# Choosing sixteen experts a head from 112 sums instead of 256, with one lookup for both keys

## The chip, the cores and the metric

The kernel runs on one core of a Trainium2 chip. The metric is the device time of one execution in microseconds (us); the time before is the median of three runs. A second source of numbers is one profiled execution of the same program, with its own time.

The engines are named as in the profile: PE (matrix multiplications, with PEld for their weight loads), DVE (vector engine), ACT (scalar engine), POOL, and SP, whose queue issues the weight transfers.

## The reference, cut to what matters

Two transformer blocks run on 256 tokens of width 1024. The second ends in a mixture of 16,384 experts, each a row of `expert_u` and a row of `expert_v`. For each of 8 heads a token has two lists of 128 scores; an expert is a pair of places, one of each list, and its score is the sum.

```python
def peer_ffn(h, w_pq, sub_keys, expert_u, expert_v):
    ...
        q = (hb @ w_pq).reshape(TOK_BLOCK, PEER_HEADS, 2, PEER_DHALF)
        s = jnp.einsum('thpd,hpnd->thpn', q, sub_keys).astype(jnp.float32)
        s1, i1 = lax.top_k(s[:, :, 0], PEER_TOPK)        # 16 best of 128
        s2, i2 = lax.top_k(s[:, :, 1], PEER_TOPK)
        cand_s = (s1[..., :, None] + s2[..., None, :]).reshape(TOK_BLOCK, PEER_HEADS, PEER_TOPK * PEER_TOPK)
        cand_i = (i1[..., :, None] * N_KEYS + i2[..., None, :]).reshape(...)
        top_s, pos = lax.top_k(cand_s, PEER_TOPK)        # 16 best of 256 sums
        idx = jnp.take_along_axis(cand_i, pos, axis=-1)
        gate = jax.nn.softmax(top_s, axis=-1).astype(hb.dtype)
        u = expert_u[idx]
        act = jax.nn.gelu(jnp.einsum('thkd,td->thk', u, hb), approximate=False)
        vv = expert_v[idx]
        return jnp.einsum('thk,thkd->td', gate * act, vv)
```

Both lists come out sorted, best first. A sum of place a of the first list and place b of the second is beaten or equalled by every sum at places no later in both lists.

## The kernel before

The kernel gathers no expert rows. It multiplies all experts with all tokens, and a dense matrix of gates (`GA`, 128 x 128 x 256: first key, second key, token) that is zero for experts that were not chosen does the selection.

**The stretch around the change.** After the first block and the attention and recurrence of the second, `lin_T(xs6, A["w_pq"], ...)` makes the queries in 16 column blocks (`evpq`, L1536, writes them to `qT`). `choose()` starts with 64 small multiplications (L1590) that give the 32 lists of scores (two halves of 128 tokens, `t`, times 8 heads times 2 keys), copied to `sc` by ACT (L1592). Then the loop over the experts begins: 64 calls of `u_pair(c, td)`, each with two slabs of 128 experts of `eu`. Later 64 pairs of slabs of `ev` follow.

**A slab.** `slab()` loads 512 KB to a buffer `raw` (three buffers), and `split()` makes two parts of it: `hi` on ACT (L327, three buffers) and `lo = raw - hi` on DVE (L329, two buffers). PE needs both: each slab of `eu` is 8 groups of three multiplications, `hi` by `hbh` (L336), `hi` by `hbl` (L337), `lo` by `hbh` (L338). A `raw` buffer is free for the next transfer when its `lo` is made.

**The choice.** `choose()` is a generator. It works on DVE alone except for its exponential, its final transposes and copies. For each half `t`:

- 16 lists: `top16` finds the 16 best of 128 and their places in five steps: MAX8 (L1560), FIND_INDEX8 (L1561), MATCH_REPLACE8 (L1562, into a scratch part of `tmp`), MAX8 (L1563), FIND_INDEX8 (L1564). In the chip each FIND and REPLACE has a short MATCH_VALUE_LOAD ahead of it.
- 8 heads: all 256 sums of the two lists (L1601), which need the two lists of that head only, and `top16` over them.
- The place of a sum, 0 to 255, is split into the two list places by a shift (L1609 or L1611) and a mask, each made into pairs of 16-bit numbers by a copy (L1612).
- The lookup of the key numbers, once for each of the two keys: compare with 0 to 15 (L1617, 2048 wide, 16 bit), multiply by the 16 key numbers (L1621), sum over 16 (L1622).

Then come the gates, and transposes and copies (`pk`, `pg`), and 32 calls of `g_group`, each of which puts the gates of 8 tokens into `GA`.

**What sets the order.** The program text interleaves the two streams: each `u_pair` is followed by up to `U_STEPS = 3` steps of `choose()` until it ends, then by as many `g_group` calls as spread 32 of them over the pairs left but for the last `U_LAST // 2`. The framework (`TileContext(nc, schedule_with_timeline_sim=True)`) turns this text into one fixed queue for each engine at compile time, with a timeline of its own; work that is ready may be put ahead of work that stands earlier in the text. On the chip each engine keeps that order. The scratch `tmp` is shared: what the second half writes there comes after what the first half's lookup does there.

Of the kernel before, what the change touches and what calls it, by code (L numbers as in the profile page):

```python
# [12 lines left out]
F16 = mybir.dt.float16  # L13
# [3 lines left out]
OP = mybir.AluOpType  # L17
AX = mybir.AxisListType
PSUM = bass.MemoryType.PSUM

P = 128
# [193 lines left out]
def body(tc, A, out):  # L215
    nc = tc.nc
    V, S, G, PE = nc.vector, nc.scalar, nc.gpsimd, nc.tensor
    es = ExitStack()
    with es:
# [14 lines left out]
        def pw(g=None):  # L234
            if g is None:
                turn[0] ^= 1
            return psw.tile([P, 512], F32, tag=f"w{turn[0] if g is None else g}", name=nm("w"), bufs=4 - LIN_PS // 2)
# [401 lines left out]
        while j < KC:  # L639
            n = 1  # L640
# [151 lines left out]
        n = MEM_PER  # L792
# [730 lines left out]
        GA = gap.tile([P, P, T], F32, name="GA")  # L1523
        view = lambda i, n, k: GA[:, i:i + n].rearrange("p a t -> p (a t)").rearrange("p (k t) -> p k t", k=k)
# [1 line left out]
        qT = GA[:, 112:128]  # L1526
        keys = view(104, 8, 16)
        sc = view(88, 16, 32)
        cand = view(72, 16, 16)
        tmp = view(64, 8, 8)  # L1530
        for j in range(2):
            nc.sync.dma_start(keys[:, 8 * j:8 * j + 8], A["keys"].rearrange("p (k n) -> p k n", k=16)[:, 8 * j:8 * j + 8])
# [12 lines left out]
        gp = es.enter_context(tc.tile_pool(name="gp", bufs=1, side="right", reuse_waits="tile"))  # L1545
# [4 lines left out]
        def carve(n, *dims):  # L1550
            flat = GA.rearrange("p a t -> p (a t)")[:, at_[0]:at_[0] + n]
            at_[0] += n
            names = "abcde"[:len(dims)]
            return flat.rearrange(f"p ({' '.join(names)}) -> p {' '.join(names)}", **dict(zip(names[:-1], dims[:-1])))

        v16 = carve(512, 2, 16, 16)
        u16 = carve(512, 2, 16, 16).bitcast(U32)

        def top16(src, scratch, vals, idx):
            V.max(vals[:, 0:8], src)  # L1560
            V.max_index(idx[:, 0:8], vals[:, 0:8], src)  # L1561
            V.match_replace(scratch, vals[:, 0:8], src, -3e38)  # L1562
            V.max(vals[:, 8:16], scratch)  # L1563
            V.max_index(idx[:, 8:16], vals[:, 8:16], scratch)  # L1564

        tv = carve(256, 2, 8, 16)
        tu = carve(256, 2, 8, 16).bitcast(U32)
        gs = carve(32, 2, 8, 2)
        ii = carve(768, 3, 2, 8, 16)
        assert at_[0] <= 64 * T  # L1570

        n16 = gp.tile([P, 2, 16, 16], F16, tag="o1", name="n16", bufs=2)
        ab = gp.tile([P, 2, 8, 16, 2], F16, tag="o1", name="ab", bufs=2)
        io = gp.tile([P, P], F16, name="io")
        G.iota(io, pattern=[[1, P]], base=0, channel_multiplier=0, allow_small_or_imprecise_dtypes=True)

# [3 lines left out]
        def twice(a):  # L1580
            return a.rearrange("p (g t) -> p g t", t=8)[:, :, :, None].to_broadcast([P, T // 8, 8, 2])

        def choose():

            for t in range(2):
                ts = slice(t * P, t * P + P)
                for g in range(4):
                    p_ = pw()
                    for i in range(4):
                        PE.matmul(p_[:, i * P:i * P + P], lhsT=qT[:, 4 * g + i, ts], rhs=keys[:, 4 * g + i], start=i == 0,  # L1590
                                  stop=i == 3, skip_group_check=True)
                    S.activation(sc[:, 16 * t + 4 * g:16 * t + 4 * g + 4], p_.rearrange("p (k n) -> p k n", k=4), AF.Copy)  # L1592
            yield
            for t in range(2):
                for k in range(16):
                    top16(sc[:, 16 * t + k], tmp[:, k % 8, 0:P], v16[:, t, k], u16[:, t, k])
                    yield
                V.tensor_copy(n16[:, t], u16[:, t])
                for h in range(8):
                    c = cand[:, 8 * t + h]  # L1600
                    V.tensor_tensor(c.rearrange("p (a b) -> p a b", a=16), v16[:, t, 2 * h, :, None].to_broadcast([P, 16, 16]),  # L1601
                                    v16[:, t, 2 * h + 1, None].to_broadcast([P, 16, 16]), op=OP.add)
                    top16(c, tmp[:, h], tv[:, t, h], tu[:, t, h])
                    yield

                pos = u16[:, t, 0:8]
                for s in range(2):
                    if s:
                        V.tensor_scalar(pos, tu[:, t], 15, None, op0=OP.bitwise_and)  # L1609
                    else:  # L1610
                        V.tensor_scalar(pos, tu[:, t], 4, None, op0=OP.logical_shift_right)  # L1611
                    V.tensor_copy(ab[:, s], pos[:, :, :, None].to_broadcast([P, 8, 16, 2]))  # L1612
                yield
                for s in range(2):
                    eq = tmp[:, 4 * s:4 * s + 4].bitcast(F16).rearrange("p a t -> p (a t)")
                    pairs = eq.rearrange("p (m a b) -> p m a b", a=8, b=2)
                    V.tensor_tensor(pairs, ab[:, s].rearrange("p h k b -> p (h k) b")[:, :, None].to_broadcast([P, P, 8, 2]),  # L1617
                                    io[:, None, 0:16].rearrange("p m (a b) -> p m a b", b=2).to_broadcast([P, P, 8, 2]),
                                    op=OP.is_equal)
                    four = eq.rearrange("p (h k a) -> p h k a", h=8, k=16)  # L1620
                    V.tensor_tensor(four, four, n16[:, t, s:16:2, None].to_broadcast([P, 8, 16, 16]), op=OP.mult)  # L1621
                    V.tensor_reduce(ii[:, s, t], four, axis=AX.X, op=OP.add)  # L1622
                    yield

            gt_ = ii[:, 2]
            V.tensor_tensor(gt_, tv, tv[:, :, :, 0:1].to_broadcast([P, 2, 8, 16]), op=OP.subtract)
            S.activation(gt_, gt_, AF.Exp)
            V.tensor_reduce(gs[:, :, :, 0], gt_, axis=AX.X, op=OP.add)
            V.reciprocal(gs[:, :, :, 1], gs[:, :, :, 0])
            V.tensor_tensor(gt_, gt_, gs[:, :, :, 1:2].to_broadcast([P, 2, 8, 16]), op=OP.mult)  # L1630
            yield
            for s in range(3):
                p_ = pw()
                for t in range(2):
                    PE.transpose(p_[:, t * P:t * P + P], ii[:, s, t].rearrange("p h k -> p (h k)"), ident)
                if s < 2:
                    S.activation(pk[:, :, s], twice(p_[:, :T]), AF.Copy)
                else:

                    S.activation(pg[:, :, 0], twice(p_[:, :T]), AF.Copy, scale=GS)  # L1640
                    V.scalar_tensor_tensor(pg[:, :, 1], twice(p_[:, :T]), GS, pg[:, :, 0], op0=OP.mult, op1=OP.subtract)
            yield
# [45 lines left out]


        steps = choose()  # L1690
        next(steps)
        ng, first = 0, None
# [70 lines left out]
```

## Time and profile before

| | us |
|---|---|
| median of 3 runs | 1503.12 (1501.41 to 1504.32) |
| time of the profiled execution | 1501.13 |
| its span, first to last instruction | 1499.4 |
| PE busy in the span | 1456.0 |
| DVE busy in the span | 1063.9 |
| ACT busy in the span | 769.0 |

All times below are counted from the start of the span; 1.7 us of the profiled execution lie outside it. The busy share of an engine is an average over stages, and the choice takes less than a tenth of the span. What the change does is to be read from the stretch in which the choice runs, about 674 to 823 us, by which engine waits there and for whom. Starts of successive instructions on an engine can lie closer together than their durations.

### The profile page before, as it was taken

The numbers are of one execution on the slowest core, as the hardware profiler recorded it, in microseconds if no ns is written. First come the engines' busy times: TensorE is split into PE (matmuls) and PEld (weight loads), VectorE is DVE, ScalarE is ACT, GpSimd is POOL, SyncE is SP. The second block draws the span as 40 slices with busy tenths as digits, with TensorE's granted clock in tenths as the row PEclk, the third lists the DMA queues.
The fourth block names the chain that finished last, engine by engine and source line by source line (L and its number), as shares of the span: only waits on it lengthen the run. The fifth ranks groups of instructions, "written<-read, shape, count | busy, mean of one in ns | idle before, by whom it ended". The sixth has DMA issues, their size and how long they took to land.

```text
span 1499.4 us, 26594 instructions
## 1 busy us (share of the span) xinstructions
PE 1456.0 (97%) x10462; PEld 1326.2 (88%) x10462; DVE 1063.9 (71%) x1871; ACT 769.0 (51%) x1242; POOL 148.2 (10%) x159
## 2 busy tenths in 40 slices
PE   8999999999999999999888999999999999999998
PEld 7888999999998867889878999999998888888886
DVE  7776676775559888489999677788875555555554
ACT  6856655665456446453434454454445444444443
POOL 7400101000225352110000000000000000000000
PEclk9999999999999979999999999999999999999999
DMA  6553444556654411164445555554545655655554
GB/s 215 167 155 113 129 153 154 184 181 188 196 179 145 138 25 40 50 197 153 151 131 158 179 159 166 159 165 156 167 159 182 187 191 184 186 192 183 187 192 141
DMA packets 75918, 237.50 MB, mean 158 GB/s; under 512 B 14608, under 2 KB 17808, under 8 KB 75792
## 3 DMA queue, kind: packets, MB, share of 16 engines
q1 hardware_dynamic: 75792, 235.79, 49.5%
q8 instruction: 82, 1.34, 0.4%
q14 instruction: 44, 0.36, 0.1%
HBM read 233.27 MB, written 2.49 MB: 157 GB/s over the span
## 4 chain that ended last, share of the span: by engine, by line
PE 86%; DVE 9%; DMA 3%; ACT 1%; issue 1%; POOL 0%; SPq 0%; DVEq 0%; ACTq 0%
PE lin L336 16%; PE lin L338 16%; PE lin L337 16%; PE w L1740 8%; PE w L1739 8%; PE w L1743 8%; DVE lo L329 2%; PE w L1661 2%; PE lin L452 1%; PE lin L453 1%; PE lin L454 1%; ACT hi L327 1%; DVE GA L1562 0%; DMA raw<-eu 0%; DVE GA L1564 0%
## 5 line engine op out<-in xcount | busy, mean ns | idle before, releaser
L329 DVE TENSOR_TENSOR lo<-raw,hi 128x1024 fp32r<-128x1024 f32 (+1 forms) x432 | 526.7, 1219 | 314.8 <-PE w L1740 99.8
L327 ACT ACTIVATE hi<-raw 128x1024 fp32r<-128x1024 f32 x437 | 458.7, 1050 | 491.2 <-PE lin L337 233.9
L338 PE MATMUL lin<-hbh,lo 128*128 128x256 f32 x1024 | 292.3, 287 | 7.9 <-DVE lo L329 7.9
L336 PE MATMUL lin<-hbh,hi 128*128 128x256 f32 x1024 | 291.8, 286 | 7.7 <-ACT hi L327 7.7
L337 PE MATMUL lin<-hbl,hi 128*128 128x256 f32 x1024 | 288.6, 283 | 0.0
L338 PEld LDWEIGHTS lin<-hbh,lo 128*128 128x128 f32 x1024 | 195.2, 191 | 10.9 <-DVE lo L329 10.4
L336 PEld LDWEIGHTS lin<-hbh,hi 128*128 128x128 f32 x1024 | 196.0, 191 | 8.9 <-ACT hi L327 8.9
L337 PEld LDWEIGHTS lin<-hbl,hi 128*128 128x128 f32 x1024 | 195.9, 191 | 0.0
L1740 PE MATMUL w<-lo,wh 128*128 128x512 f32 x504 | 159.0, 397 | 0.0
L1743 PE MATMUL w<-hi,wl 128*128 128x512 f32 x504 | 158.9, 396 | 0.0
L1739 PE MATMUL w<-hi,wh 128*128 128x512 f32 x504 | 138.6, 397 | 0.0
L1743 PEld LDWEIGHTS w<-hi,wl 128*128 128x128 f32 x504 | 94.9, 188 | 23.2
L1739 PEld LDWEIGHTS w<-hi,wh 128*128 128x128 f32 x504 | 94.9, 188 | 23.1
L1740 PEld LDWEIGHTS w<-lo,wh 128*128 128x128 f32 x504 | 94.8, 188 | 22.9
L1722 ACT ACTIVATE wh<-GA 128x512 fp32r<-128x512 f32 x64 | 40.4, 633 | 78.2 <-PE w L1740 78.2
L336 PE MATMUL lin<-xs4h,hi 128*128 128x256 f32 x256 | 72.5, 284 | 0.4 <-ACT hi L327 0.4
L338 PE MATMUL lin<-xs4h,lo 128*128 128x256 f32 x256 | 72.3, 283 | 0.0
L337 PE MATMUL lin<-al,hi 128*128 128x256 f32 x256 | 72.0, 282 | 0.0
L337 PE MATMUL lin<-xs4l,hi 128*128 128x256 f32 x256 | 71.7, 281 | 0.0
L336 PE MATMUL lin<-ah,hi 128*128 128x256 f32 x256 | 71.6, 281 | 0.0
L338 PE MATMUL lin<-ah,lo 128*128 128x256 f32 x256 | 71.2, 283 | 0.0
L498 POOL TENSOR_TENSOR sqa<-sqa,sq 128x256 f32<-128x256 f32 x37 | 37.1, 1008 | 314.3 <-ACT sq L494 300.4
(573 smaller groups left out, 3053.7 us busy)
## 6 DMA issues: line engine op xcount, KB each, us to landing
raw<-eu SPq DMA_DIRECT2D x128, 512.0 KB, 3.5
raw<-ev SPq DMA_DIRECT2D x128, 512.0 KB, 3.5
raw<-w_up SPq DMA_DIRECT2D x32, 512.0 KB, 3.5
raw<-w_down SPq DMA_DIRECT2D x32, 512.0 KB, 4.7
raw<-w_in SPq DMA_DIRECT2D x20, 512.0 KB, 3.8
raw<-w_in_s SPq DMA_DIRECT2D x16, 512.0 KB, 3.5
raw<-w_pq SPq DMA_DIRECT2D x16, 512.0 KB, 3.7
raw<-w_in_m SPq DMA_DIRECT2D x8, 512.0 KB, 3.5
```

Source lines behind the costliest of these rows:

```text
L327: S.activation(hi[:, :n], raw[:, :n], AF.Copy)
L329: eng.tensor_tensor(lo[:, :n], raw[:, :n], hi.bitcast(F32)[:, :n], op=OP.subtract)
L336: PE.matmul(ps, lhsT=lh, rhs=rh, start=start, stop=False, skip_group_check=True)
L337: PE.matmul(ps, lhsT=lh, rhs=rl, start=False, stop=False, skip_group_check=True)
L338: PE.matmul(ps, lhsT=ll, rhs=rh, start=False, stop=stop, skip_group_check=True)
L452: PE.matmul(ps, lhsT=xh, rhs=wh, start=start, stop=False)
L498: G.tensor_tensor(self.acc, self.acc, q, op=OP.add)
L1661: PE.matmul(p_[:, o_:o_ + P], lhsT=hot[:, 0, i], rhs=parts[s][:, i], start=i % 4 == 0 and s == 0, stop=i % 4 == 3 and s == 1, skip_group_c ...
L1722: S.activation(wh_, w2, AF.Copy)
L1739: PE.matmul(acc[t][d], lhsT=wh_[:, i, ts], rhs=vh[:, ds], start=c + i == 0, stop=False, skip_group_check=True)
L1740: PE.matmul(acc[t][d], lhsT=wh_[:, i, ts], rhs=vl[:, ds], start=False, stop=False, skip_group_check=True)
L1743: PE.matmul(acc[t][d], lhsT=wl_[:, i, ts], rhs=vh[:, ds], start=False, stop=False, skip_group_check=True)
```

## The change

Of the 256 sums of a head, only those are formed that can be among the 16 best: for the first four places of the first list all 16 of the second (64 sums), for the other 12 places the first 4 of the second (48 sums). `cand` holds these 112 for each head, 64 first and then 48. The sums of all 8 heads of a half are made by two instructions, after all 16 lists of the half; before, each head had an addition of its own.

The place among the 112 no longer splits by one shift and one mask. The first place is max(p >> 4, (p >> 2) - 12), and the second is p - min(16 a, 4 a + 48): three instructions on 32-bit integers and mixed types become six.

The lookup handles both keys of a half in one comparison and one multiplication, each 4096 wide in 16 bit, over the whole of `tmp`. The sum over 16 becomes a tree: three additions in place in 16 bit (8, 4 and 2 wide in each group of 16) and one that adds the last two numbers, 16 elements apart from group to group, into 32-bit `ii`. The steps of the generator grow from 27 to 29 for each half.

```diff
-        cand = view(72, 16, 16)
...
+        mt = carve(128, 8, 16)
...
+        C0, CN = 4 * 16, 4 * 16 + 12 * 4
+        cand = GA[:, 72:80].rearrange("p a t -> p (a t)")[:, :16 * CN].rearrange("p (t h n) -> p t h n", t=2, h=8)
...
+                lists = v16[:, t].rearrange("p (h s) a -> p h s a", s=2)
+                for o_, na, nb_, a0 in ((0, 4, 16, 0), (C0, 12, 4, 4)):
+                    V.tensor_tensor(cand[:, t, :, o_:o_ + na * nb_].rearrange("p h (a b) -> p h a b", a=na),
+                                    lists[:, :, 0, a0:a0 + na, None].to_broadcast([P, 8, na, nb_]),
+                                    lists[:, :, 1, None, 0:nb_].to_broadcast([P, 8, na, nb_]), op=OP.add)
+                yield
                 for h in range(8):
-                    c = cand[:, 8 * t + h]
-                    V.tensor_tensor(c.rearrange("p (a b) -> p a b", a=16), v16[:, t, 2 * h, :, None].to_broadcast([P, 16, 16]),
-                                    v16[:, t, 2 * h + 1, None].to_broadcast([P, 16, 16]), op=OP.add)
-                    top16(c, tmp[:, h], tv[:, t, h], tu[:, t, h])
+                    top16(cand[:, t, h], tmp[:, h, 0:CN], tv[:, t, h], tu[:, t, h])
                     yield
-                pos = u16[:, t, 0:8]
-                for s in range(2):
-                    if s:
-                        V.tensor_scalar(pos, tu[:, t], 15, None, op0=OP.bitwise_and)
-                    else:
-                        V.tensor_scalar(pos, tu[:, t], 4, None, op0=OP.logical_shift_right)
-                    V.tensor_copy(ab[:, s], pos[:, :, :, None].to_broadcast([P, 8, 16, 2]))
+                pos, qs = u16[:, t, 0:8], u16[:, t, 8:16]
+                two = lambda x: x[:, :, :, None].to_broadcast([P, 8, 16, 2])
+                V.tensor_scalar(pos, tu[:, t], 4, None, op0=OP.logical_shift_right)
+                V.tensor_scalar(qs, tu[:, t], 2, None, op0=OP.logical_shift_right)
+                V.scalar_tensor_tensor(ab[:, :, 0], two(qs), 12.0, two(pos), op0=OP.subtract, op1=OP.max)
+                V.tensor_scalar(mt, ab[:, :, 0, :, 0], 4.0, 48.0, op0=OP.mult, op1=OP.add)
+                V.scalar_tensor_tensor(mt, ab[:, :, 0, :, 0], 16.0, mt, op0=OP.mult, op1=OP.min)
+                V.tensor_tensor(ab[:, :, 1], two(tu[:, t]), two(mt), op=OP.subtract)
                 yield
-                for s in range(2):
-                    eq = tmp[:, 4 * s:4 * s + 4].bitcast(F16).rearrange("p a t -> p (a t)")
...
-                    V.tensor_tensor(four, four, n16[:, t, s:16:2, None].to_broadcast([P, 8, 16, 16]), op=OP.mult)
-                    V.tensor_reduce(ii[:, s, t], four, axis=AX.X, op=OP.add)
-                    yield
+                eq = tmp.bitcast(F16).rearrange("p a t -> p (a t)")
+                rows = eq.rearrange("p (m a b) -> p m a b", a=8, b=2)
+                V.tensor_tensor(rows, ab.rearrange("p h s k b -> p (h s k) b")[:, :, None].to_broadcast([P, 2 * P, 8, 2]),
+                                io[:, None, 0:16].rearrange("p m (a b) -> p m a b", b=2).to_broadcast([P, 2 * P, 8, 2]),
+                                op=OP.is_equal)
+                yield
+                four = eq.rearrange("p (h k a) -> p h k a", h=16, k=16)
+                V.tensor_tensor(four, four, n16[:, t, :, None].to_broadcast([P, 16, 16, 16]), op=OP.mult)
+                yield
+                flat = eq.rearrange("p (m a) -> p m a", a=16)
+                for w_ in (8, 4, 2):
+                    V.tensor_tensor(flat[:, :, 0:w_], flat[:, :, 0:w_], flat[:, :, w_:2 * w_], op=OP.add)
+                V.tensor_tensor(ii[:, 0:2, t].rearrange("p s h k -> p h s k"), four[:, :, :, 0].rearrange("p (h s) k -> p h s k", s=2),
+                                four[:, :, :, 1].rearrange("p (h s) k -> p h s k", s=2), op=OP.add)
+                yield
```

## Rows read from the trace of the kernel before

**Rows 1.** The page: busy time and instructions by engine; shares of the chain.
```profile
PE 1456.0 (97%) x10462; PEld 1326.2 (88%) x10462; DVE 1063.9 (71%) x1871; ACT 769.0 (51%) x1242; POOL 148.2 (10%) x159
...
PE 86%; DVE 9%; DMA 3%; ACT 1%; issue 1%; POOL 0%; SPq 0%; DVEq 0%; ACTq 0%
```

**Rows 2.** Busy time by stretch: PE, PEld, DVE, ACT, POOL; clock, DMA share, GB/s.
```profile
674.00:715.60 41.60, 40.97 (x347) 40.78 (x346) 40.79 (x174) 16.30 (x19) 0.24 (x1) 1.00 0.47 148
715.60:814.26 98.66, 84.20 (x666) 80.40 (x664) 96.83 (x303) 40.52 (x48) 0.00 (x0) 1.00 0.46 146
814.26:823.00 8.74, 7.80 (x63) 7.61 (x64) 8.04 (x7) 4.11 (x6) 0.00 (x0) 1.00 0.49 145
...
735.00:750.00 15.00, 15.00 (x125) 14.86 (x125) 14.66 (x36) 6.11 (x8) 0.00 (x0) 1.00 0.63 204
...
1000.00:1072.00 72.00, 72.00 (x670) 71.13 (x670) 60.20 (x79) 33.66 (x62) 0.00 (x0) 1.00 0.50 161
```

**Rows 3.** Waits of PE, 690 to 860 us: total, times, longest.
```profile
PE lin L338 <- DVE lo L329: 7.9, 12, 1.0
PE lin L336 <- ACT hi L327: 7.7, 5, 1.9
```

**Rows 4.** The chain in order of time: start, length, what.
```profile
785.05 1.14 DVE lo L329
786.22 3.46 DMA raw<-eu
789.78 1.07 ACT hi L327
```

**Rows 5.** PE in order of time: start, duration, instruction.
```profile
820.06 0.28 PE L338 MATMUL lin<-hbh,lo 128*128 128x256 f32 x1
820.18 0.28 PE L336 MATMUL lin<-hbh,hi 128*128 128x256 f32 x1
```

**Rows 6.** DVE groups by form, 715.60 to 814.26 us: count, busy us, mean ns.
```profile
L329 DVE TENSOR_TENSOR lo<-raw,hi 128x1024 fp32r<-128x1024 f32 x27 | 32.9, 1217 | 0.3 <-PE lin L338 0.3
L1622 DVE TENSOR_REDUCE GA<-GA 128x128 f32<-128x2048 f16 x3 | 6.8, 2279 | 0.0
L1564 DVE FIND_INDEX8 GA<-GA 128x8 uint32<-128x256 f32 x16 | 6.6, 426 | 0.0
...
L1563 DVE MAX8 GA<-GA 128x8 f32<-128x256 f32 x16 | 6.2, 418 | 0.0
L1564 DVE FIND_INDEX8 GA<-GA 128x8 uint32<-128x128 f32 x20 | 5.7, 292 | 0.0
...
L1563 DVE MAX8 GA<-GA 128x8 f32<-128x128 f32 x20 | 5.2, 285 | 0.0
...
L1617 DVE TENSOR_TENSOR GA<-ab,io 128x2048 f16<-128x2048 f16 x4 | 4.9, 1218 | 0.0
L1601 DVE TENSOR_TENSOR GA<-GA 128x256 f32<-128x256 f32 x11 | 4.5, 413 | 0.0
...
L1612 DVE CAST ab<-GA 128x256 f16<-128x256 uint32 x4 | 1.2, 288 | 0.0
...
L1611 DVE TENSOR_SCALAR GA<-GA 128x128 uint32<-128x128 uint32 x2 | 0.5, 228 | 0.0
```

**Rows 7.** DVE in order of time: four maxima of 128 together.
```profile
680.63 0.87 DVE L1563 MAX8 GA<-GA 128x8 f32<-128x128 f32 x4
```

**Rows 8.** DVE groups by form, 674 to 715.60 us: work of heads.
```profile
L1601 DVE TENSOR_TENSOR GA<-GA 128x256 f32<-128x256 f32 x6 | 2.5, 408 | 0.0
...
L1561 DVE FIND_INDEX8 GA<-GA 128x8 uint32<-128x256 f32 x4 | 1.7, 422 | 0.0
L1560 DVE MAX8 GA<-GA 128x8 f32<-128x256 f32 x4 | 1.6, 416 | 0.0
```

**Rows 9.** Splits on DVE (L329 alone) by stretch: length, busy (count).
```profile
735.65:748.58 12.93, 6.08 (x5) 0.00 (x0) 1.00 0.60 192
...
761.03:796.76 35.73, 10.93 (x9) 0.00 (x0) 1.00 0.41 127
```

More of the change, by code (lines that the diff above doesn't have):

```diff
@@ L1569, in body @@
         ii = carve(768, 3, 2, 8, 16)
+        mt = carve(128, 8, 16)
         assert at_[0] <= 64 * T
+        C0, CN = 4 * 16, 4 * 16 + 12 * 4
+        cand = GA[:, 72:80].rearrange("p a t -> p (a t)")[:, :16 * CN].rearrange("p (t h n) -> p t h n", t=2, h=8)
         n16 = gp.tile([P, 2, 16, 16], F16, tag="o1", name="n16", bufs=2)
-        ab = gp.tile([P, 2, 8, 16, 2], F16, tag="o1", name="ab", bufs=2)
+        ab = gp.tile([P, 8, 2, 16, 2], F16, tag="o1", name="ab", bufs=2)
         io = gp.tile([P, P], F16, name="io")
@@ L1607, in choose @@
-                for s in range(2):
-                    if s:
-                        V.tensor_scalar(pos, tu[:, t], 15, None, op0=OP.bitwise_and)
-                    else:
-                        V.tensor_scalar(pos, tu[:, t], 4, None, op0=OP.logical_shift_right)
-                    V.tensor_copy(ab[:, s], pos[:, :, :, None].to_broadcast([P, 8, 16, 2]))
-                yield
-                for s in range(2):
-                    eq = tmp[:, 4 * s:4 * s + 4].bitcast(F16).rearrange("p a t -> p (a t)")
[L1616 to L1620, printed above, removed]
-                    V.tensor_tensor(four, four, n16[:, t, s:16:2, None].to_broadcast([P, 8, 16, 16]), op=OP.mult)
-                    V.tensor_reduce(ii[:, s, t], four, axis=AX.X, op=OP.add)
-                    yield
+                pos, qs = u16[:, t, 0:8], u16[:, t, 8:16]
```

## The prediction

> **What bounds the kernel now.** I read the page first: PE is busy in 97% of the span and has 86% of the chain that ended last; DVE has 9% of that chain [rows 1]. A change to DVE work can pay only where DVE is in the chain, so the next view is busy time by stretch. From 715.60 to 814.26 us, where the choice shares DVE with the slab splits, DVE is busy 96.83 of 98.66 us and PE only 84.20; later, at 1000 to 1072 us, PE is busy throughout and DVE 60.20 of 72 [rows 2]. The waits of PE say for whom: for `lo`, and for `hi` [rows 3]. The chain shows that the second wait is also DVE's: a late `lo` frees its `raw` buffer late, the transfer of 3.46 us starts behind it, then comes `hi` [rows 4].
>
> Busy time understates PE's loss, because a multiplication's modelled 0.28 us covers part of a gap: successive ones start 0.12 us apart [rows 5]. So I count slabs. A slab is 24 multiplications, 24 x 0.12 = 2.88 us of PE. The stretch has 27 splits [rows 6], thus 27 x 2.88 = 77.8 us of slab work in 98.66 us: PE loses 20.9 us. That is about all the change can win, and it is DVE's queue that costs it.
>
> In that queue a split takes 1.22 us by duration but, as the next starts before it ends, about 1.13 of the queue. How much the starts gain is seen on four maxima of 0.28 us that take 0.87 together: (0.87 - 0.28) / 3 = 0.20 apart, 0.09 less than the duration [rows 6, 7]. I take 0.09 off every duration below. Under one slab PE hides 2.88 - 1.13 = 1.75 us of choice. The queue carries 98.66 - 27 x 1.13 - 1.83 idle = 66.3 us of it, 2.46 a slab. The excess, 27 x 0.71 = 19.2, and the idle 1.8 give 21.0: the same loss from the other side.
>
> **The parts, in DVE time.**
>
> Narrower search. From 256 to 128 elements a maximum falls by 418 - 285 = 133 ns and a find by 426 - 292 = 134 [rows 6], about 1.04 ns an element; I take the replacement like these. From 256 to 112 that is 0.150 us for an operation, 5 operations x 16 heads: -12.0.
>
> Sums. 16 additions at 0.41 - 0.09 = 0.32 go: -5.2. The new ones are 512 and 384 wide; by the slope from the 256-wide addition to the 1024-wide split, (1217 - 413) / 768 = 1.05 ns, they take 0.59 and 0.46 of the queue [rows 6], twice: +2.1.
>
> Comparison and multiplication. Eight at 1.22 - 0.09 = 1.13 become four of twice the width, about 2.20: -0.2.
>
> Sum over 16. Four reductions at 2.19 go: -8.8. The tree's additions are 2048, 1024, 512 and 256 wide. No row has a 16-bit addition with gaps between its groups. Near bound: like the dense 16-bit comparison, two elements a cycle (1.13, 0.60, 0.33; the last, into 32 bits, as a 32-bit addition, 0.33), 2.4 a half, +4.8. Far bound: one element a cycle as the reduction, 2.19 + 1.13 + 0.60 + 0.33 = 4.25 a half, +8.5. I take the near one: the comparison too steps through short groups, pairs of numbers, at the full rate. The Trainium skill, page "VectorE: DVE Perf Modes", section "What auto-detection actually checks", says that an operation with two tensors goes at the doubled rate if every tensor is 16-bit with step one, which would give the first three additions that rate and not the last. By that rule the sum below is -18.2, by the reduction's row -14.5.
>
> Places. Four shifts and masks (about 0.14) and four copies (0.20) go: -1.4. For each half come two shifts, two more 128-wide steps (0.14 to 0.20), and two 256-wide mixed ones (0.32, as the addition): 1.25, +2.5. They depend on each other, so each may cost its whole duration: at most +3.7. Taken: +1.1 net.
>
> The sum: -12.0 - 5.2 + 2.1 - 0.2 - 8.8 + 4.8 + 1.1 = -18.2 us of DVE time, -14.5 with the slow tree.
>
> What costs nothing: no transfer, transposition or PE step changes. The generator's 27 steps for each half become 29, so at three a pair of slabs it ends in the text in the 21st pair, not the 19th, and 32 `g_group` calls share 39 pairs, not 41. DVE has 11.8 us free in 72 there [rows 2]; if that cover went, a late `lo` would stop PE as it does in the choice.
>
> One part moves. Before the stretch, under the query projections, DVE already did six additions and four maxima and four finds of heads [rows 8]: 1.9 + 1.3 + 1.6 (with the loads ahead of the finds) = 4.8 us. Now no head can begin before the half's 16 lists are done, as one addition serves all heads, and the last scores arrive at the stretch's very start. So this work comes later. DVE is lighter by as much before 715.60, where PE idles 0.6 us by busy time [rows 2]; I give 1.5 back there, since starts lie further apart than busy time tells, and 0.6 at least.
>
> **From DVE time to the end.** This is the step that decides. The order on DVE is fixed at compile time: so much choice between two splits. Call d the choice time for a split. The loss is W x (1 - 1.75 / d) plus the wait for the exponential (1.8, unchanged). Before: W is the 66.3 and the last multiplication and reduction behind 814.26 (3.3), 69.6 us, over 29 splits, d = 2.40: 18.9 + 1.8 = 20.7 lost. After: W = 69.6 + 4.8 - 18.2 = 56.2. What is d? If the queue keeps its density, less work means fewer slots, and a slot that goes takes with it the 1.75 that PE hid: of each microsecond saved only 1 - 1.75 / 2.40 = 0.27 is won. If the slots stay and get thinner, all of it is won.
>
> The rows show both regimes. Between 761.03 and 796.76 nine splits take 35.73 us, 3.97 each, d = 2.84; between 735.65 and 748.58 five take 12.93, d = 1.46 [rows 9], and there PE loses nothing [rows 2]. In the first, plenty of independent search stands ready; in the second only the last heads, each step waiting for the one before. Of the new 56.2 us, 13.6 are lookups in pieces of 2.2 to 2.4, one to a slot: d = 2.27. For the other 42.6 I take the old mean, 2.40, somewhat thinned by the serial places and tree: d = 2.30 over all. Loss: 56.2 x (1 - 1.75 / 2.30) + 1.8 = 15.2. Gain: 20.7 - 15.2 = 5.5, and 1.5 before the stretch: 7.0.
>
> The profiled execution, 1501.1 (its span 1499.4 and 1.7 around it), becomes 1494.1. The median of the runs shown is 2.0 higher, so I add that: 1496.
>
> **Rivals.**
>
> *Thin slots.* The number of slots stays near 29 or falls little: d = 1.95 to 2.15. For it: the narrowing takes time from operations whose number stays, and steps that follow each other fill slots thinly, as at 735.65. Against it: the dense regime holds about the same time a slot whether its searches are 128 or 256 wide. At d = 2.00 the loss is 7.0 + 1.8: a gain of 11.9 + 1.5, 1490. The most that can be won is the 20.7 and 1.5.
>
> *Same.* The density rises to d = 2.50, 16.9 + 1.8 lost, which wins 2.0, and nothing comes back before the stretch; or the tree is slow (W = 59.9, at 2.40 a loss of 16.2 + 1.8, gain 2.7): about 1501, within what a measurement of this kernel tells from no change, 0.2% or 3 us.
>
> *Slower: denser slots.* One addition now makes all eight heads ready together, 40 independent searches with nothing behind them that waits. If the queue packs them as between 761.03 and 796.76, or denser, d passes its point: 56.2 x (1 - 1.75 / d) + 1.8 is the old loss and the 1.5 together at d = 2.75. At d = 3.00 it loses 23.4 + 1.8 = 25.2, net 3.0 slower: 1506. Against it: the serial parts would have to vanish from the mean; the lookups alone hold it down.
>
> *The tree at one element a cycle* is how one part of the change would not do what it says: by the reduction's row it costs 3.7 us of DVE, 1 to 2 us at the end, and is held in "same".
>
> **How the numbers follow.** Density kept or a little lower (gain 4 to 9): 0.43. Thin slots (gain 9 to 15): 0.27. Same, by density or slow tree: 0.19. Slower: 0.11. So faster 0.70, same 0.19, slower 0.11. The predicted time is that of the first case, 1496; its own range is 1494 to 1499. The range over the cases is 1487 to 1503: it takes in the thin case but for its end, and the half of "same" that lies below the old median, and leaves out about 2 in 10, most of it above.
>
> **What would show it.** Right: reductions and the 256-wide searches are gone, a find of 112 takes near 0.275 us and a maximum 0.268; the three 16-bit additions take about 1.22, 0.68 and 0.42; no head's search starts before 715 us; the stretch from there to the last lookup has about 24 splits, 3.4 us each on average, and PE's waits are still for `lo` and `hi` but shorter in total; from 830 us on the rows differ only by a shift. Wrong in size: if the splits there stand 2.9 to 3.1 us apart the thin case holds; at 3.9 and more, the dense one. Wrong in kind: PE waits after 830 us for `lo`, `GA` or `hot`, which would mean that the later `g_group` calls crowd DVE; or a tree addition of 2.2 us.

## The result and the profile after

The changed kernel takes 1489.6 us (median of 4 runs, 1486.71 to 1490.98); the kernel before, run beside it, 1503.72. The ratio is 0.990, with a 95% interval of 0.9887 to 0.9913: 14.1 us faster. Forecast were 1496 and 7 us; the measured time lies inside the range of 1487 to 1503, outside the forecast case's own 1494 to 1499, and on the "thin slots" rival's 1490.

The page of the changed kernel, busy time and shares of the chain, against [rows 1]:

```profile
PE 1456.2 (98%) x10462; PEld 1328.7 (89%) x10462; DVE 1050.3 (71%) x1861; ACT 768.9 (52%) x1240; POOL 149.9 (10%) x159
...
PE 88%; DVE 7%; DMA 2%; ACT 1%; issue 1%; POOL 0%; SPq 0%; DVEq 0%; ACTq 0%
```

PE has the same 10462 multiplications and the same busy time. DVE is busy 13.6 us less, and its share of the chain falls from 9% to 7%. Where that happens stands in the busy time by stretch (columns as in [rows 2]):

```profile
675.79:715.89 40.10, 40.10 (x336) 40.10 (x335) 36.04 (x156) 14.63 (x17) 0.24 (x1) 0.98 0.46 146
715.89:801.26 85.37, 82.99 (x679) 81.59 (x678) 82.58 (x310) 41.23 (x48) 0.00 (x0) 1.00 0.53 173
801.26:811.97 10.71, 9.55 (x78) 9.14 (x77) 10.37 (x11) 4.20 (x6) 0.00 (x0) 1.00 0.48 151
1000.00:1072.00 72.00, 72.00 (x672) 71.22 (x672) 60.16 (x79) 33.33 (x62) 0.00 (x0) 1.00 0.50 162
```

The second row runs over the same 27 slabs as the 98.66 us of before [rows 2]: 13.3 us shorter, 3.16 us a slab in place of 3.65. Counted in slabs PE loses 85.37 - 27 x 2.88 = 7.6 us there, not 20.9. In the first row DVE, with no head left to search there, has 4 us free in 40. The last row shows that nothing is given back later: PE is busy throughout and DVE has the same 60.2 us as before.

PE's waits from 660 to 860 us; the second of them lies before 690 us, so from there to 860 `hi` is not waited for at all, and `lo` 3.5 us where it was 7.9 [rows 3]:

```profile
PE lin L338 <- DVE lo L329: 3.5, 7, 1.1
PE lin L336 <- ACT hi L327: 2.5, 1, 2.5
```

DVE's groups by form, from 715.89 to 811.97 us, against [rows 6]:

```profile
L329 DVE TENSOR_TENSOR lo<-raw,hi 128x1024 fp32r<-128x1024 f32 x31 | 37.7, 1217 | 0.5 <-PE lin L338 0.3 <-issue 0.2
...
L1625 DVE TENSOR_TENSOR GA<-ab,io 128x4096 f16<-128x4096 f16 x2 | 4.6, 2292 | 0.1
L1630 DVE TENSOR_TENSOR GA<-GA,n 128x4096 f16<-128x4096 f16 x2 | 4.6, 2285 | 0.0
L1560 DVE FIND_INDEX8 GA<-GA 128x8 uint32<-128x112 f32 x16 | 4.5, 278 | 0.0
...
L1559 DVE MAX8 GA<-GA 128x8 f32<-128x112 f32 x16 | 3.0, 269 | 0.0
...
L1634 DVE TENSOR_TENSOR GA<-GA 128x2048 f16<-128x2048 f16 x2 | 2.4, 1214 | 0.0
...
L1634 DVE TENSOR_TENSOR GA<-GA 128x1024 f16<-128x1024 f16 x2 | 1.4, 686 | 0.0
...
L1605 DVE TENSOR_TENSOR GA<-GA 128x512 f32<-128x512 f32 x2 | 1.4, 682 | 0.0
...
L1634 DVE TENSOR_TENSOR GA<-GA 128x512 f16<-128x512 f16 x2 | 1.3, 662 | 0.0
...
L1635 DVE TENSOR_TENSOR GA<-GA 128x256 f32<-128x256 f16 x2 | 1.3, 650 | 0.1
...
L1605 DVE TENSOR_TENSOR GA<-GA 128x384 f32<-128x384 f32 x2 | 1.1, 548 | 0.0
```

Finds and maxima of 112 take the forecast 0.28 and 0.27 us. The first two additions of the tree (2048 and 1024 wide) come at 1.21 and 0.69 as forecast, the last two at 0.66 and 0.65 in place of 0.42. The row to look at is the first: from the stretch's start to the end of the choice there are 31 splits, not the 24 of the forecast.

### The profile page after: what moved, and what is told of

It reads as the page before. It is cut to its first block, busy times and chain, and to the rows that moved or that the text cites. A ratio compares the mean times of both kernels' runs of the same rounds, so it can differ in the third digit from the quotient of the medians.

```text
span 1487.3 us, 26587 instructions
## 1 busy us (share of the span) xinstructions
PE 1456.2 (98%) x10462; PEld 1328.7 (89%) x10462; DVE 1050.3 (71%) x1861; ACT 768.9 (52%) x1240; POOL 149.9 (10%) x159
## 4 chain that ended last, share of the span: by engine, by line
PE 88%; DVE 7%; DMA 2%; ACT 1%; issue 1%; POOL 0%; SPq 0%; DVEq 0%; ACTq 0%
PE lin L338 17%; PE lin L336 17%; PE lin L337 17%; PE w L1754 8%; PE w L1753 8%; PE w L1757 8%; PE w L1675 2%; DVE lo L329 2%; PE lin L452 1%; PE lin L453 1%; PE lin L454 1%; DMA raw<-w_pq 0%; PE w L1102 0%; PE w L1169 0%; ACT hi L327 0%
## 5 line engine op out<-in xcount | busy, mean ns | idle before, releaser
L329 DVE TENSOR_TENSOR lo<-raw,hi 128x1024 fp32r<-128x1024 f32 (+1 forms) x432 | 528.5, 1223 | 312.5 <-PE lin L338 102.6
```

The costliest lines, as they stand in the source:

```text
L329: eng.tensor_tensor(lo[:, :n], raw[:, :n], hi.bitcast(F32)[:, :n], op=OP.subtract)
```

## The experiments

One measure serves them all. Take the whole choice, from its first maximum to the end of its last lookup instruction: its length T, and the number n of splits that stand between the two in DVE's queue. PE needs 2.88 us for each slab, so T - 2.88 n is what PE does not spend on slabs there, called the loss below. Not all of it is waiting: 56 of PE's 64 small multiplications for the choice lie in T, and in the changed kernel they take 5.0 us, counted from each start to the next start on PE. Ten of them in the kernel before, with the multiplication that starts 1.03 us after the first of them:

```profile
701.96 1.28 PE L1590 MATMUL w<-GA 128*128 128x128 f32 x10
702.99 0.37 PE L338 MATMUL lin<-xs6h,lo 128*128 128x256 f32 x1
```

In the one kernel below whose PE waits for nothing in T, the loss is 9.7. Said from DVE's side: choice work and idle time cost their length one to one, and each split that stands inside the choice gives 2.88 - 1.13 = 1.75 us back. "Choice time" below is what the choice's own instructions take of DVE in T, each from its start to the next instruction's start (where a gap behind it is longer than 0.15 us, only to its own end); beside them and the splits stand 6 to 12 us of idle time and of a few other instructions.

The splits alone over that stretch (length, DVE busy with the count; a split that only overlaps the edge is counted too), the kernel before:

```profile
673.99:819.95 145.96, 48.76 (x41) 0.00 (x0) 1.00 0.46 147
```

and the changed kernel:

```profile
675.79:811.70 135.91, 51.08 (x42) 0.00 (x0) 0.99 0.51 163
```

Before: 40 splits stand there (the 41st starts behind the last reduction, just before that ends), so 145.96 - 115.2 = 30.8 us of loss. After: 42 splits, 135.91 - 121.0 = 14.9. There are 16 us less choice time (94.5 to 78.2), yet two more splits between it.

**The narrow search alone**, with the two lookups and reductions of before:

```diff
+        ab = gp.tile([P, 2, 8, 16, 2], F16, tag="o1", name="ab", bufs=2)
...
-                V.tensor_tensor(four, four, n16[:, t, :, None].to_broadcast([P, 16, 16, 16]), op=OP.mult)
...
+                for s in range(2):
+                    eq = tmp[:, 4 * s:4 * s + 4].bitcast(F16).rearrange("p a t -> p (a t)")
...
+                    V.tensor_tensor(four, four, n16[:, t, s:16:2, None].to_broadcast([P, 8, 16, 16]), op=OP.mult)
+                    V.tensor_reduce(ii[:, s, t], four, axis=AX.X, op=OP.add)
+                    yield
```

> The changed kernel with the old lookups: 112 sums, two additions for all heads of a half and the six place steps stay, but each key has its own comparison, multiplication and reduction, 2048 wide. Against the kernel before DVE has 12.0 + 3.1 - 1.1 = 14.0 us less. Thin slots (the number of splits during the choice stays, a microsecond of DVE is nearly one at the end): 10 to 12 us faster than before, about 1492. Density kept (slots go, 0.27 of a microsecond): 4 us faster, about 1500. Long pieces (what cost the time were the reductions and their neighbours in one slot): 0 to 3 us faster, 1501 to 1504.

```profile
674.50:808.55 134.05, 49.78 (x42) 0.00 (x0) 1.00 0.52 165
```

Measured 1489.82 us, ratio 0.991 (0.9895 to 0.9925) to a before of 1504.15: 14.3 us, all that the whole change gains. Choice time is 80.8 us, 13.7 less than before, and 41 splits still stand in it: the loss falls to 16.0. The instructions became shorter, their order kept its splits, so nearly every microsecond saved arrived. That is the thin case, and it speaks against a density that keeps its time a slot.

**The new lookup alone**, with 256 sums a head:

```diff
-                for o_, na, nb_, a0 in ((0, 4, 16, 0), (C0, 12, 4, 4)):
...
+                    c = cand[:, 8 * t + h]
+                    V.tensor_tensor(c.rearrange("p (a b) -> p a b", a=16), v16[:, t, 2 * h, :, None].to_broadcast([P, 16, 16]),
+                                    v16[:, t, 2 * h + 1, None].to_broadcast([P, 16, 16]), op=OP.add)
+                    top16(c, tmp[:, h], tv[:, t, h], tu[:, t, h])
```

> The kernel before with the new lookup alone: 256 sums a head with an addition for each head, shift and mask, but one comparison and one multiplication 4096 wide and the tree. DVE has 8.8 + 0.2 - 4.8 = 4.2 us less. Thin slots: 3 to 4 us faster than before, about 1500. Density kept: 1 to 2 us, about 1502. Long pieces: most of the 14.1 us, 9 to 12 us faster, about 1493.

```profile
675.19:824.20 149.01, 51.03 (x42) 0.00 (x0) 0.98 0.46 149
```

Measured 1501.42, ratio 0.9982 (0.9973 to 0.9992): 2.7 us, far from the 9 to 12 that long pieces would have given. Choice time falls by 2.2, and the choice has 42 splits: loss 28.0, 2.8 less than before. On top of the narrow search the same lookup adds nothing that the end shows (14.1 us gained beside 14.3). Its loss is 1.1 smaller, but the choice begins at 675.79 where it began at 674.50. These starts lie anywhere from 672.8 to 675.8 in the kernels here; why was not pursued.

**Two reductions in place of the tree**, all else as changed:

```diff
-                for w_ in (8, 4, 2):
-                    V.tensor_tensor(flat[:, :, 0:w_], flat[:, :, 0:w_], flat[:, :, w_:2 * w_], op=OP.add)
...
+                for s in range(2):
+                    V.tensor_reduce(ii[:, s, t], four.rearrange("p (h s) k a -> p h s k a", s=2)[:, :, s], axis=AX.X, op=OP.add)
```

> The changed kernel with two reductions of 2048 for a half in place of the tree. By its rows in the changed kernel the tree takes 1.13 + 0.75 + 0.70 + 0.82 = 3.4 us of the queue a half, the reductions 4.4, so DVE has about 2 us more in all. Thin slots: 2 us slower than the changed kernel, about 1491.5. Density kept: 0.5 us, 1490. Long pieces: nothing, as pieces of 2.2 us are in the changed kernel already.

Measured 1497.71, ratio 0.9959 (0.9945 to 0.9972): 8.1 us slower than with the tree, though choice time is only 2.5 us longer (80.7). The splits alone, and then DVE in order of time around the first lookup's end (start, duration, instruction):

```profile
674.36:806.48 132.12, 46.01 (x39) 0.00 (x0) 0.99 0.48 156
```

```profile
748.71 1.22 DVE L329 TENSOR_TENSOR lo<-raw,hi 128x1024 fp32r<-128x1024 f32 x1
749.85 4.47 DVE L1633 TENSOR_REDUCE GA<-GA 128x128 f32<-128x2048 f16 x2
754.24 1.22 DVE L329 TENSOR_TENSOR lo<-raw,hi 128x1024 fp32r<-128x1024 f32 x1
```

The same place with the tree, in the changed kernel:

```profile
751.47 1.22 DVE L329 TENSOR_TENSOR lo<-raw,hi 128x1024 fp32r<-128x1024 f32 x1
752.61 1.22 DVE L1634 TENSOR_TENSOR GA<-GA 128x2048 f16<-128x2048 f16 x1
753.74 1.22 DVE L329 TENSOR_TENSOR lo<-raw,hi 128x1024 fp32r<-128x1024 f32 x1
754.88 0.69 DVE L1634 TENSOR_TENSOR GA<-GA 128x1024 f16<-128x1024 f16 x1
755.78 1.22 DVE L329 TENSOR_TENSOR lo<-raw,hi 128x1024 fp32r<-128x1024 f32 x1 [0.21 <-issue]
756.92 0.67 DVE L1634 TENSOR_TENSOR GA<-GA 128x512 f16<-128x512 f16 x1
757.62 0.67 DVE L1635 TENSOR_TENSOR GA<-GA 128x256 f32<-128x256 f16 x1
```

The tree's additions wait for one another, and the compile-time order puts a split into the first two of the three joints, in both halves (not into the last, between 512 and 256). The two reductions need nothing of each other and stand back to back, 4.47 us without a split. Over the whole choice that is 38 splits for 42, and the four are those of the joints. Their loss is 7.8 us larger: 2.5 of time, and four splits less, 4 x 1.75 = 7.0; together 9.5, less 1.7 that DVE idles less.

**Priority for the splits**, a marker in the program text that should raise them in the layout:

```diff
-                wh, wl = slab(A["eu"][c + i])
+                raw = load(A["eu"][c + i])
+                with tc.high_priority(offset=400):
+                    wh, wl = split(raw)
```

> The changed kernel with the splits of the eu slabs given priority over the choice when the queues are laid out; the work is the same. If the loss that is left is splits that stand behind too much choice in DVE's queue, the splits move forward and PE's waits there, 8.8 for lo and 4.2 for hi in the changed kernel, fall to a few: 1481 to 1485. If the layout puts each split where its own timeline has it ready and priority changes only ties, it stays at 1489 within 2 us.

```profile
675.01:812.67 137.66, 50.77 (x42) 0.00 (x0) 0.99 0.51 161
```

Measured 1489.89, ratio 0.9905 (0.989 to 0.9921): 42 splits as without it. DVE's order differs in places, but the marker adds no split, so the run says nothing on what more splits are worth; the last three kernels do that in another way.

**Width or number.** Two kernels add DVE time to the changed one in different ways. The first searches 256 columns again, of which 144 hold padding:

```diff
+        cand = view(72, 16, 16).rearrange("p (t h) n -> p t h n", t=2)
+        for t in range(2):
+            G.memset(cand[:, t, :, CN:], -3e38)
...
-                    top16(cand[:, t, h], tmp[:, h, 0:CN], tv[:, t, h], tu[:, t, h])
+                    top16(cand[:, t, h], tmp[:, h], tv[:, t, h], tu[:, t, h])
```

> The changed kernel with its searches over 256 places, of which 144 are filled with a very small number once on POOL: the same instructions in number, 80 of them 144 elements wider, 12.0 us more DVE time, and nothing else. Thin slots (the choice keeps its number of splits, DVE time goes to the end one to one): 1501, 11 to 12 us slower than the changed kernel. Density kept: 3 us slower, 1493. If the gain came from the shared additions or from a better order and not from width: within 2 us of 1489.6.

```profile
675.20:823.81 148.61, 52.17 (x43) 0.00 (x0) 0.99 0.48 153
```

The second does every head's narrow search twice:

```diff
+                    for _ in range(2):
+                        top16(cand[:, t, h], tmp[:, h, 0:CN], tv[:, t, h], tu[:, t, h])
```

> The changed kernel with each search over the 112 sums made twice, 80 instructions more and the same result: at 1.08 us of the queue for a search (rows of the changed kernel: 0.176 for each maximum and replacement, 0.185 and 0.06 of load for a find) 17.3 us more DVE time. Density kept: the second searches get slots of their own, 5 us slower, 1495. Thin slots: 15 to 17 us slower, about 1505, where the instructions go into slots that are there. A slot longer by whole instructions may also be laid out with more splits: between the two.

```profile
673.53:834.54 161.01, 58.41 (x48) 0.00 (x0) 0.99 0.50 158
```

Wide: 1498.79, ratio 0.9963 (0.995 to 0.9976). Choice time grows by 12.5 us (90.7), splits by one: 9.2 us slower. Twice: 1495.31, ratio 0.9943 (0.993 to 0.9956). Choice time grows by 17.9 (96.1), splits by six: only 5.7 slower. More work cost less, because it came as 80 more searching instructions, and the order laid splits among them; six splits take back 10.5 us, one takes back 1.75. So in these kernels the number of splits in the choice goes with how many instructions it has and how they follow each other, and hardly with how wide they are.

**Additions of each head's own**, so that heads may be searched before all lists are done:

```diff
-                for o_, na, nb_, a0 in ((0, 4, 16, 0), (C0, 12, 4, 4)):
-                    V.tensor_tensor(cand[:, t, :, o_:o_ + na * nb_].rearrange("p h (a b) -> p h a b", a=na),
...
                 for h in range(8):
+                    for o_, na, nb_, a0 in ((0, 4, 16, 0), (C0, 12, 4, 4)):
+                        V.tensor_tensor(cand[:, t, h, o_:o_ + na * nb_].rearrange("p (a b) -> p a b", a=na),
...
```

> The changed kernel with two additions for each head in that head's step, 64 and 48 wide, in place of the two for all heads: 16 x 0.24 = 3.8 against 2.1 us of DVE, but a head can again be searched before all lists of the half are done, under the query projections. If barring that was a cost (4.8 us of such work before): 1 to 3 us faster than the changed kernel, 1487 to 1488.5. If it was none: 1 to 2 us slower, 1491.

```profile
675.49:809.36 133.87, 48.81 (x40) 0.00 (x0) 0.99 0.50 158
```

Measured 1491.88, ratio 0.9918 (0.9902 to 0.9933), 2.3 us behind the changed kernel, with intervals that overlap: choice time 2.1 longer, 40 splits. Heads are searched before 715 us again (four maxima and four finds of 112 stand there), but that gains nothing. That one addition bars all heads until the lists are done cost nothing on balance.

**Reductions in short pieces.** If the reductions of the third experiment hurt because they are long, eight pieces of 0.6 us for each half should heal it:

```diff
+                for h in range(0, 8, 2):
+                    for s in range(2):
+                        V.tensor_reduce(ii[:, s, t, h:h + 2], four.rearrange("p (h s) k a -> p h s k a", s=2)[:, h:h + 2, s], axis=AX.X, op=OP.add)
```

> The kernel with reductions in place of the tree (8 us slower than the changed one, where 2 us of DVE were expected), its two reductions of 2048 for a half cut to eight of 512: 0.7 us more DVE time in all. If two pieces of 2.2 us behind each other between two splits made the loss, shorter pieces let a split in between and it falls to 1491 to 1493; if the amount of DVE time or something else did, it stays at 1497 to 1499.

Measured 1496.70, ratio 0.9952 (0.9938 to 0.9966); no cure. The splits alone, 39 without the one at the edge, and then DVE in order of time at the first lookup's end:

```profile
672.77:806.90 134.13, 47.37 (x40) 0.00 (x0) 0.98 0.49 154
```

```profile
747.18 1.22 DVE L329 TENSOR_TENSOR lo<-raw,hi 128x1024 fp32r<-128x1024 f32 x1
748.32 4.24 DVE L1634 TENSOR_REDUCE GA<-GA 128x32 f32<-128x512 f16 x7
752.48 1.21 DVE L329 TENSOR_TENSOR lo<-raw,hi 128x1024 fp32r<-128x1024 f32 x1
```

Seven of the eight pieces stand together, in both halves. Here pieces that do not depend on each other are packed between two splits though each is short, so the idea that long instructions keep splits out has fallen. What sets the tree apart is that each step waits for the one before. That this is the reason is argued from these three kernels; waiting alone does not do it, as the tree's last joint has no split.

**One piece behind each split.** The last three lay down the order by hand. The block in `tc.issue_after(x)` comes after x in DVE's fixed queue; both are DVE's, so what changes is the order. `behind` names, for steps of `choose()`, the split (counted from the first of `eu`) that a step stands behind: one head or one piece of a lookup for each split. The changed kernel with it:

```diff
-            eng.tensor_tensor(lo[:, :n], raw[:, :n], hi.bitcast(F32)[:, :n], op=OP.subtract)
+            los.append(eng.tensor_tensor(lo[:, :n], raw[:, :n], hi.bitcast(F32)[:, :n], op=OP.subtract))
...
+        behind = {16 + j: 3 + j for j in range(13)} | {45 + j: 22 + j for j in range(13)}
...
-                    if next(steps, mix) is mix:
+                    at = behind.get(done_)
+                    with tc.issue_after(los[base + at].ins) if at is not None else ExitStack():
+                        end = next(steps, mix) is mix
+                    done_ += 1
+                    if end:
```

> The changed kernel with the same DVE work, but from the additions on each step of a half may stand only behind a split of its own in DVE's queue: one head, or one piece of the lookup, to a split. The queue then has four splits more between the first search and the end of the tree, 46 for 42. If the loss is DVE time less 1.75 us a split, 7 us less, bounded by what the changed kernel still loses (about 7.5) and less what DVE then idles: 1483 to 1486. If slots were no cause, only DVE time: 1489 to 1490.

```profile
675.33:817.18 141.85, 55.85 (x46) 0.00 (x0) 1.00 0.54 171
```

Measured 1484.89, ratio 0.9879 (0.9861 to 0.9897). The same instructions, 81.3 us of choice time, and 46 splits: loss 9.4. The next one also cuts the lookup's comparison and multiplication in two, each half behind a split of its own:

```diff
+                for d in range(2):
+                    V.tensor_tensor(rows[:, P * d:P * d + P], ab[:, 4 * d:4 * d + 4].rearrange("p h s k b -> p (h s k) b")[:, :, None].to_broadcast([P, P, 8, 2]),
...
+                for d in range(2):
+                    q = four[:, 8 * d:8 * d + 8]
+                    V.tensor_tensor(q, q, n16[:, t, 8 * d:8 * d + 8, None].to_broadcast([P, 8, 16, 16]), op=OP.mult)
+                    yield
...
+        behind = {14: 3, 15: 3} | {16 + j: 4 + j for j in range(15)} | {47 + j: 24 + j for j in range(15)}
```

> As the one before, and the 4096-wide comparison and multiplication are each made in two halves of 2048, each behind a split of its own, and the last two lists of the first half behind the third split: 0.3 us more DVE time, seven splits more than the changed kernel, no slot of the lookup above 1.75 us but the one with the gates. Loss by slots: 1481 to 1484. If long pieces are hidden by the buffers anyway: as the one before. DVE time only: 1490.

Splits alone, and then all engines, over the choice:

```profile
674.71:825.51 150.80, 59.62 (x49) 0.00 (x0) 0.99 0.53 172
674.71:825.51 150.80, 150.80 (x1250) 150.47 (x1249) 140.76 (x484) 69.39 (x80) 0.24 (x1) 0.99 0.53 172
```

Measured 1482.52, ratio 0.9863 (0.9846 to 0.988): the fastest here, ahead of both kernels. The choice is longer than in any but two others, and PE no longer waits for it: PE is busy in all of the 150.80 us, and its trace lists no wait from 674 to 826 us. The loss of 9.7 that the measure still gives is thus work or lies at the edges of T: 5.0 are the small multiplications, and 1.4 the half slab by which PE's 1188 slab multiplications in T (49.5 slabs) exceed the 49 splits; the last 3 were not taken apart. The choice time of a split is 83.0 / 49 = 1.69, under the 1.75 that PE hides. The run before, with 1.77, was all but there: its loss is 9.4, PE waits 1.2 us in T, and the two intervals overlap. So it is not shown that the halves won the 2.4 us between the two.

Last, the kernel before with the same order by hand (one head or piece for each split) and none of the change:

```diff
+        behind = {18 + j: 4 + j for j in range(9)} | {43 + j: 21 + j for j in range(11)}
```

> The kernel before, with none of the change: 256 sums, two lookups, reductions; only its heads and lookups are laid out one step to a split in the same way. DVE time is the same 94.5 us, the queue has seven splits more up to the last reduction. If DVE time less 1.75 us a split is the loss: 7 x 1.75 = 12 us less, minus what DVE idles, 1492 to 1496, most of what the change won. If what counts is DVE time alone: 1503 to 1504.

```profile
674.78:829.38 154.60, 57.18 (x48) 0.00 (x0) 0.99 0.51 162
```

Measured 1492.32, ratio 0.9924 (0.991 to 0.9938). With all of the 256 sums and both lookups (choice time 94.7, as before), 47 splits in place of 40 win 11.3 us of the change's 14.1.

All kernels on the one measure; the profiled time is that of the execution the other columns are from:

| kernel | start of the choice | T | splits n | loss T - 2.88 n | choice time | profiled time |
|---|---|---|---|---|---|---|
| before | 673.99 | 145.96 | 40 | 30.8 | 94.5 | 1501.13 |
| changed | 675.79 | 135.91 | 42 | 14.9 | 78.2 | 1489.05 |
| narrow search alone | 674.50 | 134.05 | 41 | 16.0 | 80.8 | 1486.89 |
| new lookup alone | 675.19 | 149.01 | 42 | 28.0 | 92.3 | 1501.38 |
| two reductions | 674.36 | 132.12 | 38 | 22.7 | 80.7 | 1494.54 |
| priority | 675.01 | 137.66 | 42 | 16.7 | 78.4 | 1489.87 |
| wide | 675.20 | 148.61 | 43 | 24.8 | 90.7 | 1498.79 |
| twice | 673.53 | 161.01 | 48 | 22.8 | 96.1 | 1494.38 |
| own additions | 675.49 | 133.87 | 40 | 18.7 | 80.3 | 1492.40 |
| short reductions | 672.77 | 134.13 | 39 | 21.8 | 81.5 | 1493.30 |
| laid by hand | 675.33 | 141.85 | 46 | 9.4 | 81.3 | 1483.19 |
| by hand, halves | 674.71 | 150.80 | 49 | 9.7 | 83.0 | 1482.32 |
| before, by hand | 674.78 | 154.60 | 47 | 19.2 | 94.7 | 1491.29 |

Profiled time less start less loss is 796.3 to 798.8 us in all thirteen, while the loss goes from 9.4 to 30.8. So the start of the choice and its loss give the end to within 2.5 us. The starts, 3 us apart, stay unexplained. T alone does not: the kernel with the shortest choice is 8 us slower than the changed one, and the fastest kernel has one of the longest.

## Why the prediction was right, and its size too small

*What bounds the kernel* held: DVE's queue in the choice costs PE its time, PE is busy throughout behind it as before, and the count in slabs is the right way to see it.

*The parts, in DVE time* nearly held. The narrower search with its sums and places was put at -12.0 - 5.2 + 2.1 + 1.1 = -14.0, and alone it took 13.7. The lookup with the tree was put at -0.2 - 8.8 + 4.8 = -4.2 and gave 2.2 alone and 2.6 on top of the search. The two narrow steps of the tree explain 2 x (0.24 + 0.23) = 0.9 of the difference; the rival of a tree as slow as the reduction (2.19 us for the 2048-wide step) did not come. In all 16.3 of the 18.2 us.

*The part that moves* held: no head's search stands before 715 us, DVE is lighter there, and the 12 splits up to the stretch, counted one by one in both traces, take 42.23 us in place of 43.75, the 1.5 forecast. What was not foreseen is that the choice begins 1.8 us later, for a cause that lies before it and is not known, so that the stretch begins 0.3 us later than before.

*From DVE time to the end* is where the size went wrong, in d, the choice time for a split. The form of the sum is right. From 715.89 to 811.97 us DVE works 92.95 us, idles 3.1 and does 31 splits; less 31 x 1.13 that is W = 57.9, forecast 56.2. But d is 57.9 / 31 = 1.87, not 2.30. Then 57.9 x (1 - 1.75 / 1.87) + 3.1 = 6.8 us are lost, which is what the count gives, 96.08 - 31 x 2.88 = 6.8. Forecast were 15.2, with 24 splits. Against the 20.7 of before that gains 13.9, less the 0.3 of the later start 13.6; measured 14.1.

The reason given for d was that the order keeps its density in time, as the dense regime of [rows 9] held about as much time a slot with searches of 128 as of 256. The runs show the other: in these kernels the splits go with the number and the chaining of instructions. The narrowing left their number (41 splits, where 40 were), the tree put dependent steps in place of reductions that stand together. The rival *thin slots* named both ("operations whose number stays", "steps that follow each other") and its 1490 is the time that came; its 3.16 us a split is just over the 2.9 to 3.1 it was to be known by. That its time came so exactly is partly luck: it stood on W = 56.2 and d = 2.00, where the trace has 57.9 and 1.87, and on 1.5 us won before the stretch, which the late start took back. Its slots were to stay or fall a little; in the stretch they rose, from 29 to the last lookup to 31. *Denser slots* would have come from all heads' being ready together; undoing that with own additions left fewer splits (40 for 42), not more.

Still open is why the compile-time order lets in a split where it does. Its own timeline isn't in the trace; the runs only show the outcome.

## What to carry to other kernels

Where a filler shares an in-order engine with a producer that feeds the bound engine, count the producer's instructions inside the filler's stretch: here each was worth 1.75 us, as much as that much work removed. A microsecond off an instruction arrives whole if the order keeps its producers; taking instructions away, or turning a chain into independent ones, can take producers out with it and cost more than it saves. Laying the order by hand, one piece of filler behind each producer, won 11.3 us with no work removed, against 14.1 for the whole change; with both, and no more choice time for a split than PE hides, PE no longer waited.

## What the runs showed of the hardware

The last three additions of the tree, 1024, 512 and 256 wide, all step through 256 short rows (4, 2 and 1 numbers of every 16), and take nearly the same, 686, 662 and 650 ns; the first, with 256 rows of 8, takes 1214. The Trainium skill, page "VectorE: DVE Perf Modes", section "What auto-detection actually checks", gives the doubled rate to an operation whose tensors are all 16-bit with step one; that agrees with 1214 and 686 (the reduction of 2048 numbers takes 2279 [rows 6]), but by the slope between these two the 512-wide one would take 0.42 us, and it took 0.66. So here the measurement decides against the doubled rate for rows of two, and from four numbers to a row down to one the time hardly fell with the numbers. All four additions have 256 rows, so that the time goes with the number of rows is not shown. Rows of other lengths or distances were not measured.
